# Output stage of a Fourier + SSD mixer: one y bank that also holds the sum of squares, three banks for decay exponents, Fourier rows first

## The chip, the core and the metric

The kernel runs on one core of one Trainium2 chip. The metric is device time in microseconds (us). A core has a matmul engine (TensorE, PE in the profile; its weight loads are PEld), three engines for everything else (VectorE is DVE, ScalarE is ACT, GpSimd is POOL) and a queue engine (SyncE, SP) that issues all DMAs of this kernel. Each engine works through its own list of instructions in a fixed order and waits on semaphores for the others. Matmul results go to PSUM, which has eight banks of 2 KB for each of the 128 partitions: a bank holds 512 float32 numbers per partition.

## The reference, cut to what matters

One layer works on 2048 latent tokens (and 256 context tokens ahead of them) of width 1024. One input projection feeds two groups: a Fourier group (512 channels, a two-dimensional DFT, a linear map, a SiLU gate) and an SSD group (1536 channels: 24 heads of 64 in four groups of six, a Mamba-2 scan in both directions, gated RMSNorm per group of 384 channels). Both are put side by side and multiplied by one output matrix. The change lies in the end of the SSD path and in the output product:

```python
lmat  = jnp.exp(segsum(a))                       # decay matrix of a chunk of 128 tokens, per head
y_diag = einsum(cb, lmat, xc)                    # inside the chunk
y_off  = einsum(cc, prev_states, exp(a_cum))     # from the state before the chunk
y = y_f + flip(y_b) + d_skip * xs
gated = y.reshape(b, l, g, r * p) * silu(zs)     # 4 groups of 384
gated = gated * rsqrt(mean(gated * gated, axis=-1, keepdims=True) + EPS)
ssd = gated.reshape(b, l, 1536) * norm_w
x = x + gate[:, None] * (concatenate([four, ssd], -1) @ w_out)
return rmsnorm(x, final_norm_w)
```

## The kernel before, in words

Earlier stages project the input, convolve, run the backward scan and the Fourier group, and leave their results in DRAM: the gated Fourier rows are in `fm_d`, the split output matrix in `wo_d`. The last stage, here called the output stage, takes the 16 chunks of 128 tokens in order, and in each chunk the four groups: 64 units, u = 4c + g. All matrix products of float32 data are made of three matmuls on a high and a low part (`split`: ScalarE copies the high part, another engine subtracts it for the low part, line 72).

A unit goes through six functions:

- `s1` loads the decay data and makes the decay exponents: in each of two halves of three heads two matmuls of 128x384, one for each direction, into two tiles `parg` (L1079); VectorE merges the second into the first under a mask (L1081), ScalarE takes the exponential (L1083), and after both halves VectorE multiplies by `cb` (L1084). The result is `w`.
- `s2` splits the running state `hf` and multiplies it with C: three matmuls into `pyo` (L1115 to L1117), scaled by VectorE into `ts` (L1119); GpSimd adds the stored backward part (L1120).
- `s3` makes the unit's contribution to the state, three matmuls into `pst4` (L1136 to L1138), and adds it to `hf` (L1141 on GpSimd, L1142 on VectorE). The last chunk has none.
- `s4` makes y, transposed, in the tile `py` of 128x384: six matmuls of x with `w` (L1151) and three transposes that add `ts` (L1154). VectorE gates it into `gt` (L1157), ScalarE squares (L1159), VectorE adds the three blocks into `s0` (L1161).
- `s5` makes the gated RMSNorm: a matmul of `s0` with a matrix of ones puts the sum of squares into `pn`, 128x128 (L1167, recorded as two passes); ScalarE takes logarithm, exponential and square (L1170, L1171, L1172), VectorE refines the reciprocal root in place in `pn` (L1173, L1174) and multiplies `gt` by it (L1176); `gt` is then split into `mh` and `ml` (L68 on ScalarE, L72 on GpSimd).
- `s6` makes the output product of the unit, 24 matmuls of 128x512 (L1210 to L1212): four blocks of rows (q) by two halves of the output (i) by three parts. Three blocks are the unit's SSD rows, the fourth its Fourier rows `fm`, which `fm_half` loads from `fm_d` for two units at a time into one buffer `fr` (L1186) and splits. `po0` and `po1` gather over the four units of a chunk. At g = 3 the gate (L1224), the residual (L1225, GpSimd), the sum of squares of the final norm (Square with an accumulator, L1227) and the store follow.

The program calls them for u = 0 ... 65 in this order: `s1(u+1)`, `s2(u+1)`, `s3(u)`, `s4(u)`, `s5(u-1)`, `s6(u-2)`. The units' order in the queues of the engines is not this one: a scheduler (`schedule_with_timeline_sim=True`, L1369) plays the program with its own durations and lists each engine's instructions as they come free. The lists are fixed before the run.

PSUM tiles come from the pool `ps2` by tag. A tile of a tag with one buffer can be written again when the last reader of the tile before it is done. Before the change the eight banks are: two for `parg`, two for `po0` and `po1`, two that `pyo` and `pst4` take in turn, one for `py`, one for `pn`.

Of the kernel before, what the change touches and what calls it, by code (L numbers as in the profile page):

```python
# [9 lines left out]
F32 = mybir.dt.float32  # L10
# [3 lines left out]
ALU = mybir.AluOpType  # L14
# [4 lines left out]
P = 128  # L19
# [30 lines left out]
def mixer_layer(ctx: ExitStack, tc: tile.TileContext, A: dict, out: bass.AP, taps=None):  # L50
    nc = tc.nc
    mm = nc.tensor.matmul

    def pool(name, bufs=1, space=None, stack=ctx, side=None):
        kw = {"space": space} if space is not None else {}
        if side is not None:
            kw["side"] = side
        if space != DRAM:
            kw["reuse_waits"] = "tile"
        return stack.enter_context(tc.tile_pool(name=name, bufs=bufs, **kw))  # L60

    def load(dst, src):
        return nc.sync.dma_start(out=dst, in_=src).ins
# [80 lines left out]
    ps = pool("ps01", stack=pps, space=PSUM)  # L144
# [7 lines left out]
    def main_psum():  # L152
        return ps.tile([P, 512], F32, name="pj", tag="mm", bufs=MAIN["bufs"])
# [202 lines left out]
    with ExitStack() as pu:  # L356
# [144 lines left out]
        for n2 in range(16):  # L501
            if n2 == 1:
                ctx_block()
            po = main_psum()
# [6 lines left out]
            with tc.issue_after(mu):  # L511
                if n2 in dt_work:
                    fn, i = dt_work[n2]
# [18 lines left out]
    with ExitStack() as pc_:  # L532
        ps = pool("psc", stack=pc_, space=PSUM)
# [164 lines left out]
    ps = pool("ps01b", stack=p1, space=PSUM)  # L698
# [72 lines left out]
    with ExitStack() as psc:  # L771
# [66 lines left out]
        for n, a in enumerate(seq):  # L838
            if n + AHEAD < len(seq):
                side.append((0.0, scan_prep(*seq[n + AHEAD])))  # L840
            dr, c, g = a
# [204 lines left out]
    ps = pool("ps2", space=PSUM)  # L1046
    fo["new"] = lambda: ps.tile([P, 512], F32, name="pft", tag="out", bufs=2)
    pre2 = preload(LNEXP)
    units = {}

    def s1(u):
        c, g = divmod(u, G)
        d = units[u] = {}
        if g == 0:
            sml = wa1.tile([P, 3, H], F32, name="sml4", tag="sml")
            load(sml, smf_d[:, c])
        else:
            sml = units[u - 1]["sml"]
        d["sml"] = sml
        r, l = rt[u % 2], lt[u % 2]  # L1060
        cs = slice(c * P, c * P + P)
        for dr in range(2):
            hsl = slice(dr * H + g * HG, dr * H + (g + 1) * HG)
            load(r[32 * dr + 12:32 * dr + 14, :].rearrange("o (h w) -> o h w", w=P).bitcast(F32),
                 cum_d[:, hsl, cs].bitcast(F32))
            for s in range(2):
                load(l[32 * dr + 6 * s:32 * dr + 6 * s + 6, dr].bitcast(F32), q_d[s, hsl, cs].bitcast(F32))
        cb = wa1.tile([P, P], F32, name="cb", tag="cb")
        load(cb, cb_d[c, :, g])
        chl = wa1.tile([P, 2, P], F32R, name="chl", tag="chl")  # L1070
        load(chl[:].bitcast(F32), chl_d[c, :, g].bitcast(F32))
        d["chl"] = chl
        w = wa1.tile([P, HG, P], F32, name="w", tag="w")
        for h2 in range(2):
            cols = slice(384 * h2, 384 * h2 + 384)
            pa = []
            for dr in range(2):
                po = ps.tile([P, 3, P], F32, name="parg", tag="arg", bufs=2)
                mm(po, l[:, dr], r[:, cols], start=True, stop=True)  # L1079
                pa.append(po)  # L1080
            nc.vector.copy_predicated(out=pa[0], mask=msk[:].unsqueeze(1).broadcast_to([P, 3, P]), data=pa[1])  # L1081
            with tc.issue_after(pre2):
                d["exp"] = nc.scalar.activation(w[:, 3 * h2:3 * h2 + 3], pa[0], AF.Exp).ins  # L1083
        nc.vector.tensor_tensor(out=w, in0=w, in1=cb[:].unsqueeze(1).broadcast_to([P, HG, P]), op=ALU.mult)  # L1084
        d["w"] = w

    for u in range(2):
        s1(u)
# [56 lines left out]
    def s4(u):  # L1145
        c, g = divmod(u, G)
        d = units[u]
        py = ps.tile([P, 3, P], F32, name="py", tag="yT", bufs=1)
        for h in range(HG):
            o = 64 * (h % 2)  # L1150
            mm(py[o:o + 64, h // 2, :], d["x"][:, h], d["w"][:, h], start=(h < 2), stop=False, skip_group_check=True)  # L1151
        tsf = d["ts"][:].rearrange("p h w -> p (h w)")
        for j in range(3):
            mm(py[:, j, :], tsf[:, j * P:(j + 1) * P], ident, is_transpose=True, start=False, stop=(j == 2),  # L1154
               skip_group_check=True)
        gt = wk.tile([P, 3, P], F32, name="gt", tag="gt")
        nc.vector.scalar_tensor_tensor(out=gt, in0=py, scalar=-1.0, in1=d["zs"], op0=ALU.mult, op1=ALU.mult)  # L1157
        sq = wk.tile([P, 3, P], F32, name="sq4", tag="sq", bufs=1)
        nc.scalar.activation(sq, gt, AF.Square)  # L1159
        s0 = wk.tile([P, P], F32, name="s0", tag="s0", bufs=1)  # L1160
        nc.vector.tensor_reduce(out=s0, in_=sq[:].rearrange("p j l -> p l j"), axis=AX.X, op=ALU.add)  # L1161
        d["gt"], d["sq"] = gt, s0

    def s5(u):
        d = units[u]
        pn = ps.tile([P, P], F32, name="pn", tag="misc", bufs=1)
        mm(pn, ones, d["sq"], start=True, stop=True)  # L1167
        rs = wk.tile([P, P], F32, name="rs4", tag="rs", bufs=1)
        tt = wk.tile([P, P], F32, name="tt", tag="tt", bufs=1)
        nc.scalar.activation(rs, pn, AF.Ln, bias=eps_t[:, 0:1], scale=1.0 / GW)  # L1170
        nc.scalar.activation(rs, rs, AF.Exp, scale=-0.5)  # L1171
        nc.scalar.activation(tt, rs, AF.Square, scale=math.sqrt(0.5 / GW))  # L1172
        nc.vector.scalar_tensor_tensor(out=pn, in0=pn, scalar=EPS * GW, in1=tt, op0=ALU.add, op1=ALU.mult)  # L1173
        nc.vector.scalar_tensor_tensor(out=pn, in0=pn, scalar=1.5, in1=rs, op0=ALU.subtract, op1=ALU.mult)  # L1174
        mx = d["gt"]
        nc.vector.tensor_tensor(out=mx, in0=mx, in1=pn[:].unsqueeze(1).broadcast_to([P, 3, P]), op=ALU.mult)  # L1176
        mh = wk.tile([P, 3, P], F32R, name="mh", tag="mh", bufs=2)
        ml = wk.tile([P, 3, P], F32R, name="ml", tag="ml", bufs=2)
        split(mh, ml, mx, nc.gpsimd)
        d["mh"], d["ml"] = mh, ml  # L1180
# [10 lines left out]
    def s6(u):  # L1191
        c, g = divmod(u, G)
        d = units.pop(u)
# [8 lines left out]
        fm = ost[c, g // 2]  # L1202
        if g % 2 == 1 and u + 1 < NU:
            fm_half(*divmod(u // 2 + 1, 2))
        ops = [(4 + 3 * g + j, d["mh"][:, j], d["ml"][:, j]) for j in range(3)] + [(g, fm[:, 0, g % 2], fm[:, 1, g % 2])]
        for i, q in [(i, q) for i in range(2) for q in range(4)] if (u > NU-2) else [(i, q) for q in range(4) for i in range(2)]:
                k, a, b = ops[q]
                wh, wl = wos[k]
                po = ost["po"][i]
                mm(po, a, wh[:, i], start=(g == 0 and q == 0), stop=False)  # L1210
                mm(po, a, wl[:, i], start=False, stop=False)  # L1211
                mm(po, b, wh[:, i], start=False, stop=(g == 3 and q == 3))  # L1212
# [27 lines left out]
        for i in range(2):  # L1240
            sl = slice(512 * i, 512 * i + 512)
            nc.vector.scalar_tensor_tensor(out=xr[i], in0=xr[i], scalar=rs[:, 0:1], in1=fnw[:, sl], op0=ALU.mult,
                                           op1=ALU.mult)
            store(out[c * P:(c + 1) * P, sl], xr[i])

    NU = NCH * G
# [126 lines left out]
```

## Time and profile before

| | |
|---|---|
| median of three runs | 1903.54 us (1899.87 to 1904.05) |
| the profiled execution | 1907.05 us, its span 1905.3 us |
| TensorE busy | 1810.8 us, 95% of the span |
| VectorE, GpSimd, ScalarE busy | 1259.1, 904.0, 874.9 us |
| granted TensorE clock, mean of the span | 0.978 |
| output stage: first `pn` to the end of the span | 1271.1 to 1905.3 us |
| first po with Fourier rows behind it to the last matmul | about 1306 to 1897 us |

A row of operations by line reads: line, engine, operation, output<-inputs, shape, count | busy time, mean ns of one | idle time of the engine just before them, and what ended most of it. A row of waits reads: who waited <- who released it: total us, times, longest. A row of windows reads: window, its length, busy time of TensorE with the number of instructions, the clock that it was granted, the share of the DMA engines, GB/s. A row of the timeline reads: start, duration, engine, line, operation, shape, and in brackets the idle time before it and what ended it. A row by one line of the program reads: shortest/median/longest ns, first start to last end. A span of 0.39 us for a matmul overlaps with its neighbours', since they are pipelined.

### The profile page before, as it was taken

How to read it: one execution, taken by the hardware profiler on the slowest of the kernel's cores; microseconds unless marked ns; L12 is line 12 of the kernel's file. 1: busy time of each engine (PE TensorE's matmuls, PEld its weight loads, DVE VectorE, ACT ScalarE, POOL GpSimd, SP SyncE). 2: the span in 40 equal slices, each digit the busy share in tenths (PEclk: the TensorE clock that was granted, in tenths of full speed). 3: DMA queues.
4: the chain of work that ended last, by engine and by line, in shares of the span. 5: the costliest groups of instructions: out<-in, count | busy, mean ns of one | idle time of the engine just before them, and what ended most of it. 6: DMA issues, size and time to landing. Idle time of an engine off the chain costs nothing.

```text
span 1905.3 us, 28132 instructions
## 1 busy us (share of the span) xinstructions
PE 1810.8 (95%) x9142; PEld 1495.8 (79%) x9142; DVE 1259.1 (66%) x1809; ACT 874.9 (46%) x1968; POOL 904.0 (47%) x791
## 2 busy tenths in 40 slices
PE   7989999999999999999999999957999999999997
PEld 3779988888888888788888877845778777777875
DVE  4744578888898887556666622334677777767865
ACT  4532244445445445347666643312444444434443
POOL 2320034223124133178788723235777777668742
PEclk9999999999999999999999999977999999999999
DMA  8332345445446245467777764786444444444441
GB/s 306 127 95 78 96 135 169 144 130 160 128 125 194 90 138 159 143 196 216 209 218 212 221 232 136 245 277 208 123 146 149 130 132 135 148 122 137 145 136 48
DMA packets 291332, 301.80 MB, mean 158 GB/s; under 512 B 34098, under 2 KB 242066, under 8 KB 290675
## 3 DMA queue, kind: packets, MB, share of 16 engines
q1 hardware_dynamic: 291186, 300.01, 50.6%
q8 instruction: 73, 1.20, 0.3%
q14 instruction: 73, 0.59, 0.1%
HBM read 196.82 MB, written 103.10 MB: 157 GB/s over the span
## 4 chain that ended last, share of the span: by engine, by line
PE 72%; DMA 9%; POOL 4%; DVE 3%; issue 2%; ACT 2%; SPq 1%; POOLq 0%; ACTq 0%; DVEq 0%
PE pj L178 11%; PE pj L177 11%; PE pj L176 11%; PE po L1212 6%; PE po L1210 6%; PE po L1211 6%; PE py L1151 2%; PE parg L1079 2%; POOL sl L72 2%; PE pj L508 1%; PE pj L509 1%; PE pj L510 1%; PE py L1154 1%; DMA ev<-in_wout 1%; PE ptr L569 1%
## 5 line engine op out<-in xcount | busy, mean ns | idle before, releaser
L178 PE MATMUL pj<-hh,wl 128*128 128x512 f32 x1152 | 453.9, 394 | 0.8 <-POOL wl L72 0.8
L176 PE MATMUL pj<-hh,wh 128*128 128x512 f32 x1152 | 450.7, 395 | 3.9 <-ACT img L68 2.1
L177 PE MATMUL pj<-hl,wh 128*128 128x512 f32 x1152 | 453.3, 393 | 0.0
L636 DVE SCALAR_TENSOR_TENSOR pacc<-img,c_convw,pacc 128x1024 f32<-128x1024 f32 x320 | 410.4, 1288 | 60.2 <-ACT pacc L633 50.7
L72 POOL TENSOR_TENSOR wl<-raw,wh 128x1024 fp32r<-128x1024 f32 x48 | 115.6, 2409 | 348.7 <-ACT wh L68 296.2
L178 PEld LDWEIGHTS pj<-hh,wl 128*128 128x128 f32 x1152 | 217.2, 189 | 48.3 <-issue 1.6
L176 PEld LDWEIGHTS pj<-hh,wh 128*128 128x128 f32 x1152 | 217.4, 189 | 46.7 <-ACT img L68 3.2
L177 PEld LDWEIGHTS pj<-hl,wh 128*128 128x128 f32 x1152 | 217.4, 189 | 40.3 <-issue 1.0
L807 ACT ACTIVATE xd<-xt,smb 128x64 f32<-128x64 f32 x384 | 100.9, 336 | 80.1 <-POOL yb L811 78.7
L1210 PE MATMUL po<-hl,mh 128*128 128x512 f32 x288 | 118.7, 412 | 1.0 <-DVE og L1224 0.6
L1211 PE MATMUL po<-hh,mh 128*128 128x512 f32 x288 | 115.0, 399 | 0.0
L1081 DVE COPY_PREDICATED parg<-msk,parg 128x384 f32<-128x384 uint8 x128 | 71.2, 556 | 65.9 <-PE parg L1079 65.4
L1212 PE MATMUL po<-hl,ml 128*128 128x512 f32 x288 | 110.6, 403 | 2.5 <-POOL ml L72 2.4
L1083 ACT ACTIVATE w<-parg 128x384 f32<-128x384 f32 x128 | 62.2, 486 | 108.3 <-DVE parg L1081 108.0
L72 DVE TENSOR_TENSOR xl<-xw,xh 128x384 fp32r<-128x384 f32 x76 | 63.7, 842 | 59.4 <-ACT xh L68 58.0
L1120 POOL TENSOR_TENSOR ts<-ts,yb 128x384 f32<-128x384 f32 x64 | 73.3, 1145 | 57.9 <-issue 30.4
L1079 PE MATMUL parg<-rt,lt 128*128 128x384 f32 x256 | 87.7, 371 | 11.8 <-DMA lt<-q_d 7.5
L72 POOL TENSOR_TENSOR ml<-gt,mh 128x384 fp32r<-128x384 f32 x64 | 68.2, 1065 | 58.9 <-ACT mh L68 55.5
L68 ACT ACTIVATE xh<-xw 128x384 fp32r<-128x384 f32 x136 | 70.0, 516 | 50.2 <-PE pst L1138 17.0
L1084 DVE TENSOR_TENSOR w<-w,cb 128x768 f32<-128x768 f32 x64 | 81.0, 1265 | 12.0 <-ACT w L1083 10.8
L72 POOL TENSOR_TENSOR sl<-ev,sh 128x512 fp32r<-128x512 f32 x32 | 42.4, 1324 | 89.6 <-DMA wo_d<-sl 36.0
L72 DVE TENSOR_TENSOR sl<-hbk,sh 128x384 fp32r<-128x384 f32 x64 | 60.0, 939 | 37.4 <-ACT sh L68 37.3
(388 smaller groups left out, 4131.9 us busy)
## 6 DMA issues: line engine op xcount, KB each, us to landing
raw<-in_win SPq DMA_DIRECT2D x48, 512.0 KB
xt<-xtok_d SPq DMA_DIRECT2D x80, 192.0 KB
xtok_d<-tk SPq DMA_DIRECT2D x48, 256.0 KB
zsT_d<-ev SPq DMA_DIRECT2D x48, 256.0 KB
yb_d<-yb SPq DMA_DIRECT2D x64, 192.0 KB
yb<-yb_d SPq DMA_DIRECT2D x64, 192.0 KB
zs<-zsT_d SPq DMA_DIRECT2D x64, 192.0 KB
xg<-xtok_d SPq DMA_DIRECT2D x64, 192.0 KB
```

The source lines that it names most:

```text
L72: (lo_engine or nc.vector).tensor_tensor(out=lo, in0=src, in1=hi.bitcast(F32), op=ALU.subtract)
L176: mm(po, wh[:, k], a, start=(k == 0), stop=False)
L177: mm(po, wh[:, k], b, start=False, stop=False)
L178: done["mm"] = mm(po, wl[:, k], a, start=False, stop=(k == KT - 1)).ins
L636: nc.vector.scalar_tensor_tensor(out=acc, in0=im[:, r0 + dy:r0 + dy + 16, dx:dx + GRID_W], scalar=tap(t), in1=acc, op0=ALU.mult, op1=ALU.add)
L807: nc.scalar.activation(xd[:, h], d["x"][:, h], AF.Copy, scale=smb[:, 3, c, g * HG + h:g * HG + h + 1])
L1079: mm(po, l[:, dr], r[:, cols], start=True, stop=True)
L1084: nc.vector.tensor_tensor(out=w, in0=w, in1=cb[:].unsqueeze(1).broadcast_to([P, HG, P]), op=ALU.mult)
L1120: nc.gpsimd.tensor_tensor(out=ts, in0=ts, in1=yb, op=ALU.add)
L1210: mm(po, a, wh[:, i], start=(g == 0 and q == 0), stop=False)
L1211: mm(po, a, wl[:, i], start=False, stop=False)
L1212: mm(po, b, wh[:, i], start=False, stop=(g == 3 and q == 3))
```

## The change

There are three edits in the output stage.

1. The two `parg` tiles of a half get tags of their own. The first direction's tile (`arg0`, which VectorE merges into and ScalarE reads) has two buffers, the second's (`arg1`, which only VectorE reads) has one: three banks in place of two.
2. The bank comes from `pn`. The `py` tile, so far 384 of the 512 columns of its bank, is made 512 wide, and `pn` of unit u becomes the fourth quarter of the `py` tile of unit u+1. The y tag still has one buffer. The last unit takes a fresh y tile for its `pn`.
3. In `s6` the Fourier rows are the first of the four blocks instead of the last; in the last unit both halves' Fourier rows come first, then the rest half by half.

```diff
@@ s1
-                po = ps.tile([P, 3, P], F32, name="parg", tag="arg", bufs=2)
+                po = ps.tile([P, 3, P], F32, name="parg", tag=f"arg{dr}", bufs=2 - dr)
                 mm(po, l[:, dr], r[:, cols], start=True, stop=True)
@@ s4
-        py = ps.tile([P, 3, P], F32, name="py", tag="yT", bufs=1)
+        py = d["py"] = ps.tile([P, 4, P], F32, name="py", tag="yT", bufs=1)
...
-        nc.vector.scalar_tensor_tensor(out=gt, in0=py, scalar=-1.0, in1=d["zs"], op0=ALU.mult, op1=ALU.mult)
+        nc.vector.scalar_tensor_tensor(out=gt, in0=py[:, :3], scalar=-1.0, in1=d["zs"], op0=ALU.mult, op1=ALU.mult)
@@ s5
-        pn = ps.tile([P, P], F32, name="pn", tag="misc", bufs=1)
+        pn = (units[u + 1]["py"] if u + 1 < NU else ps.tile([P, 4, P], F32, name="py", tag="yT", bufs=1))[:, 3]
         mm(pn, ones, d["sq"], start=True, stop=True)
...
-        nc.vector.tensor_tensor(out=mx, in0=mx, in1=pn[:].unsqueeze(1).broadcast_to([P, 3, P]), op=ALU.mult)
+        nc.vector.tensor_tensor(out=mx, in0=mx, in1=pn.unsqueeze(1).broadcast_to([P, 3, P]), op=ALU.mult)
@@ s6
-        ops = [(4 + 3 * g + j, d["mh"][:, j], d["ml"][:, j]) for j in range(3)] + [(g, fm[:, 0, g % 2], fm[:, 1, g % 2])]
-        for i, q in [(i, q) for i in range(2) for q in range(4)] if (u > NU-2) else [(i, q) for q in range(4) for i in range(2)]:
+        ops = [(g, fm[:, 0, g % 2], fm[:, 1, g % 2])] + [(4 + 3 * g + j, d["mh"][:, j], d["ml"][:, j]) for j in range(3)]
+        for i, q in ([(0, 0), (1, 0)] + [(i, q) for i in range(2) for q in range(1, 4)] if u > NU - 2
+                     else [(i, q) for q in range(4) for i in range(2)]):
```

Lines after 1202 stand one lower in the changed kernel. The scheduler makes new lists from this. Numbers behind a name in the following rows tell one tile of that name from another, so that a tile can be followed; `x6` is the count of equal rows.

TensorE in the middle of the stage, before: `pn` of unit 25 has its own tile, and `py_14639` of unit 26 follows further down.

```order
L1211 MATMUL po1_14670<-hh_85,mh_14527 128x512
L1167 MATMUL pn_14655<-s0_14515,c_ones_11274 128x128
L1079 MATMUL parg_14597<-rt1_11281,lt1_11283 128x384
L1115 MATMUL pyo_14848<-sh4_14849,chl_14823 128x384
L1116 MATMUL pyo_14848<-sl4_14850,chl_14823 128x384
L1117 MATMUL pyo_14848<-sh4_14849,chl_14823 128x384
L1151 MATMUL py_14639<-w_14456,xg_14474 64x128 x6
L1154 MATMUL py_14639<-c_ident_77,ts_14478 128x128 x3
```

The next `py` tile, unit 27's, is written some 30 rows further down. TensorE at the same place, changed: `pn` of unit 25 is written into `py_14614`, the tile of unit 26, and the next `py` tile in the same bank, `py_14726` of unit 27, is written five rows behind it.

```order
L1079 MATMUL parg_14807<-rt1_11281,lt1_11283 128x384
L1167 MATMUL py_14614<-s0_14491,c_ones_11274 128x128
L1115 MATMUL pyo_14929<-sh4_14930,chl_14904 128x384
L1116 MATMUL pyo_14929<-sl4_14931,chl_14904 128x384
L1117 MATMUL pyo_14929<-sh4_14930,chl_14904 128x384
L1079 MATMUL parg_14909<-rt0_11280,lt0_11282 128x384
L1151 MATMUL py_14726<-w_14569,xg_14587 64x128 x6
L1154 MATMUL py_14726<-c_ident_77,ts_14591 128x128 x3
```

So `pn` of a unit moved from ahead of the next unit's `py` to behind it, and the `py` of the unit after that follows after four to thirteen matmuls, depending on the unit.

ScalarE between the reading of the sum of squares and the high part of the normalised `gt`, changed, a unit with four matmuls in between (L68 is the copy of a high part, `sh4` of the state, `mh` of `gt`):

```order
L1170 ACTIVATE rs4_14157<-py_14140,eps_t_78 128x128
L1171 ACTIVATE rs4_14157<-rs4_14157 128x128
L68 ACTIVATE sh4_14705<-hf_6671 128x384
L1172 ACTIVATE tt_14158<-rs4_14157 128x128
L68 ACTIVATE mh_14165<-gt_14013 128x384
```

VectorE around the same steps, changed, for the `pn` of unit 26 (`py_14726` is its tile, `gt_14624` what it normalises):

```order
L1161 TENSOR_REDUCE s0_14740<-sq4_14738 128x128
L1142 TENSOR_TENSOR hf_6671<-hf_6671,pst4_14945 128x384
L1081 COPY_PREDICATED parg_14913<-msk8_11276,parg_14915 128x384
L1173 SCALAR_TENSOR_TENSOR py_14726<-py_14726,tt_14744 128x128
L1174 SCALAR_TENSOR_TENSOR py_14726<-py_14726,rs4_14743 128x128
L1176 TENSOR_TENSOR gt_14624<-gt_14624,py_14726 128x384
L1119 TENSOR_TENSOR ts_14928<-pyo_14929,sml4_14669 128x384
```

Other work of both engines stands between the steps on one sum of squares: a copy of the state's high part on ScalarE, the state's sum and a merge of exponents on VectorE.

TensorE where the stage begins, before: the sum of squares of unit 0 and the first output products stand around unit 1's `py`.

```order
L1151 MATMUL py<-w,xg 64x128 x6
L1154 MATMUL py<-c_ident,ts 128x128 x3
L1079 MATMUL parg<-rt_11281,lt_11283 128x384 x2
L1167 MATMUL pn<-s_11616,c_ones 128x128
L1151 MATMUL py<-w,xg 64x128 x6
L1154 MATMUL py<-c_ident,ts 128x128 x3
L1210 MATMUL po_11796<-hl,mh 128x512
L1211 MATMUL po_11796<-hh,mh 128x512
L1210 MATMUL po_11797<-hl,mh 128x512
```

The same place, changed:

```order
L1079 MATMUL parg<-rt_11281,lt_11283 128x384 x3
L1151 MATMUL py<-w,xg 64x128 x6
L1154 MATMUL py<-c_ident,ts 128x128 x3
L1151 MATMUL py<-w,xg 64x128 x6
L1154 MATMUL py<-c_ident,ts 128x128 x3
L1167 MATMUL py<-s_11616,c_ones 128x128
L1079 MATMUL parg<-rt_11280,lt_11282 128x384 x3
L1115 MATMUL pyo<-sh_11652,chl 128x384
L1116 MATMUL pyo<-sl_11653,chl 128x384
L1117 MATMUL pyo<-sh_11652,chl 128x384
```

The 18 output matmuls of unit 0's SSD rows no longer stand here: they come behind those of its Fourier rows.

## The prediction

> Times are microseconds of the profiled execution; u counts the 64 units of the output stage, four to a chunk.
>
> **What bounds the kernel now.** I read the page, then the output stage by windows, then what TensorE waited for there.
>
> ```profile
> span 1905.3 us, 28132 instructions
> PE 1810.8 (95%) x9142; PEld 1495.8 (79%) x9142; DVE 1259.1 (66%) x1809; ACT 874.9 (46%) x1968; POOL 904.0 (47%) x791
> ```
> ```profile
> 1306.00:1897.00 591.00, 573.62 (x3146) 0.99 0.44 131
> ```
> ```profile
> PE pst L1136 <- DVE ts L1119: 5.6, 9, 1.5
> PE po L1212 <- POOL ml L72: 2.4, 2, 1.7
> PE parg L1079 <- DVE parg L1081: 2.3, 2, 1.8
> PE py L1151 <- DVE w L1084: 1.8, 3, 0.8
> PE parg L1079 <- ACT w L1083: 0.4, 2, 0.3
> ```
>
> The windows row gives the stretch, its length, TensorE's busy time and its clock; the wait rows give total, times and longest of that stretch. From the first steady unit to the last matmul TensorE is busy 573.6 of 591.0: the stage is bound by its matmuls. Only 17.4 are idle, and the rows that the change could touch (parg on VectorE 2.3, on ScalarE 0.4, ml 2.4) make 5.1. With all waits gone the gain would end at 17. So the question is what new wait the shared bank brings.
>
> **The chain in the shared bank.** Last unit, nothing competing:
>
> ```profile
> 1885.15 0.38 PE L1167 MATMUL pn<-s,c_ones 128*128 128x128 f32 x2
> ```
> ```profile
> 1885.63 0.37 ACT L1170 ACTIVATE rs<-pn,eps_t 128x128 f32<-128x128 f32 x1 [2.08 <-PE pn L1167]
> 1886.03 0.31 ACT L1171 ACTIVATE rs<-rs 128x128 f32<-128x128 f32 x1
> 1886.37 0.31 ACT L1172 ACTIVATE tt<-rs 128x128 f32<-128x128 f32 x1
> ```
> ```profile
> 1886.72 0.30 DVE L1173 SCALAR_TENSOR_TENSOR pn<-pn,tt 128x128 f32<-128x128 f32 x1 [3.72 <-ACT tt L1172]
> 1887.05 0.30 DVE L1174 SCALAR_TENSOR_TENSOR pn<-pn,rs 128x128 f32<-128x128 f32 x1
> 1887.38 0.55 DVE L1176 TENSOR_TENSOR gt<-gt,pn 128x384 f32<-128x384 f32 x1
> ```
> ```profile
> L1167 PE MATMUL pn<-s,c_ones x128: 270/273/580, 1271.1 to 1885.3; 128*128 128x128 f32 x128
> L1176 DVE TENSOR_TENSOR gt<-gt,pn x64: 535/552/555, 1273.7 to 1887.4; 128x384 f32<-128x384 f32 x64
> ```
>
> From pn's start to the end of L1176, the last reader of pn, is 1887.93 - 1885.15 = 2.78: call it L. Pairing the 64 starts of L1167 with the 64 ends of L1176 (first and last in the two rows above), L is 2.73 at least, 4.24 in the median, 7.19 at most; the difference is queueing on ScalarE and VectorE. Now nothing waits for it: pn has its own bank, and the next use is a unit away.
>
> **The change, part by part.** With pn in the fourth quarter of a y tile and one y bank, the y tile of unit u+2 can't be written until L1176 of unit u has read the sum that lies in the tile of u+1. The first matmul of py(u+2) takes that wait, and with it everything behind it in TensorE's queue: the 24 po of a unit, parg, pst, pyo. In the changed order pn(u) stands behind py(u+1) and directly ahead of py(u+2). What lies between them is cover. Prices of it:
>
> ```profile
> 1361.85 0.39 PE L1211 MATMUL po<-hh,mh 128*128 128x512 f32 x1
> 1362.08 0.39 PE L1210 MATMUL po<-hl,mh 128*128 128x512 f32 x1
> 1370.11 0.33 PE L1116 MATMUL pyo<-sl,chl 128*128 128x384 f32 x1
> 1370.29 0.34 PE L1117 MATMUL pyo<-sh,chl 128*128 128x384 f32 x1
> ```
>
> Start to start, a 512-wide matmul costs 0.23 and a 384-wide one (pyo, pst, parg) 0.18. Counting the changed order, between pn(u) and py(u+2) stand 4 narrow ones (13 units: 0.70), 5 narrow (6: 0.88), 9 narrow (14: 1.58), 5 narrow and 6 wide (14: 2.28), 7 narrow and 6 wide (6: 2.69); the other nine are the entry and the end. Over the 59 units behind the entry the cover is 1.54 on average. A stall is L - 0.2 - cover (pn's own slot is 0.23, the handover about 0.04, as between tt's end and L1173's start above).
>
> How large L gets there I take from the changed orders of ScalarE and VectorE, with these means:
>
> ```profile
> L1081 DVE COPY_PREDICATED parg<-msk,parg 128x384 f32<-128x384 uint8 x121 | 67.3, 556 | 54.5 <-PE parg L1079 54.1
> L1142 DVE TENSOR_TENSOR hf<-hf,pst 128x384 f32<-128x384 f32 x57 | 31.2, 547 | 2.3 <-PE pst L1138 2.0
> L68 ACT ACTIVATE sh<-hf 128x384 fp32r<-128x384 f32 x58 | 30.1, 519 | 22.1 <-PE pyo L1117 18.0 <-DVE hf L1142 3.5
> L72 DVE TENSOR_TENSOR fm<-fr,fm 128x256 fp32r<-128x256 f32 x32 | 22.4, 701 | 17.7 <-ACT fm L68 17.1 <-DMA cb<-cb_d 0.5
> L1225 POOL TENSOR_TENSOR xr<-xr,og 128x512 f32<-128x512 f32 x30 | 41.5, 1382 | 13.1 <-DVE og L1224 13.1
> L1227 ACT ACTIVATE og<-xr 128x512 f32<-128x512 f32 x30 | 18.8, 628 | 11.7 <-POOL xr L1225 11.6
> ```
>
> With 4 narrow ones, a copy sh (0.52) stands between the chain's second and third activation: L = 2.78 + 0.55 = 3.3. With 9, the hf add and a parg copy stand ahead of L1173 and wait for pst and parg that follow pn (hf can start 1.15 after pn; 1.15 + 0.55 + 0.56 + 1.2 for the three VectorE steps = 3.5), and where the fm remainder (0.70) stands there too, 4.2. With 6 wide ones (a chunk's last unit) the Square L1227 (0.63 and its read of the sum) waits for GpSimd's xr (1.38) before the chain's second step: 4.25. Weighted: L = 3.8. Stall 3.8 - 0.2 - 1.54 = 2.06, times 59 = 122; the last two pn follow each other, 3 more: **+125**. Bounds: the quiet chain everywhere, by classes 13 x 1.89 + 6 x 1.71 + 14 x 1.01 + 14 x 0.31, some 10 for the end: +64; the median of before everywhere, 2.5 x 59: +150.
>
> TensorE also pays in clock:
>
> ```profile
> 1345.80:1349.21 3.41, 1.71 (x10) 1.00 0.41 139
> 1349.21:1352.62 3.41, 2.84 (x9) 0.50 0.85 272
> 1352.62:1356.04 3.42, 3.42 (x18) 0.50 0.57 171
> 1666.65:1670.06 3.41, 1.72 (x8) 1.00 0.24 70
> 1670.06:1673.48 3.42, 3.42 (x10) 0.50 0.48 131
> 1857.79:1861.20 3.41, 1.88 (x10) 1.00 0.41 119
> 1861.20:1864.61 3.41, 3.41 (x17) 1.00 0.07 19
> ```
> ```profile
> 1669.33 0.74 PE L1212 MATMUL po<-hl,ml 128*128 128x512 f32 x2 [1.67 <-POOL ml L72]
> ```
>
> The clock steps on a grid of 3.41. Twice a window only 1.7 busy was followed by a halved one; one 1.88 busy was not. One idle stretch of 1.67 was enough. A stall of 2.06 puts 1.65 or more into one window in (3.41 + 2.06 - 3.3)/3.41 = 0.64 of its positions, and a halved window costs half of 3.41: 0.64 x 1.7 x 59 = **+64**. Bounds: 0 (never) and, if every second window is halved too as at 1352.62, about +100. The Trainium skill ("TensorE: Matmul & The Clock Gate", section "HAM oscillation — how this bites in real kernels") gives the rule that idle gaps should stay under about 3.4 microseconds. By that rule alone these stalls would leave the clock alone; the trace disagrees with a halving after 1.67.
>
> The **third parg bank** and the **Fourier rows first** can remove at most the waits: all 16 of the stage vanish behind the longer ones (-16, with their halved windows (6.8 + 3.4)/2 = 5 more); neither end is below that. The instructions are the same in number and shape.
>
> At the **entry** before uses a hole:
>
> ```profile
> 1274.81 0.80 PE L1210 MATMUL po<-hl,mh 128*128 128x512 f32 x1 [0.39 <-ACT mh L68]
> 1280.10 0.39 PE L1212 MATMUL po<-hl,ml 128*128 128x512 f32 x1
> 1282.69 0.68 PE L1079 MATMUL parg<-rt,lt 128*128 128x384 f32 x2 [1.98 <-DMA lt<-q_d]
> ```
> ```profile
> 1301.57 0.42 SPq L63 DMA_DIRECT2D fr<-fm_d  x1
> ```
>
> Unit 0's 18 mh and ml matmuls run from 1274.81 to 1280.3, while SP's queue of loads holds the rest back. With the Fourier rows first they stand behind fr, issued at 1301.57 in the same place of SP's queue. They are paid later: 18 x 0.23 = **+4** (0 to 6).
>
> Sum: 1907.05 (the profiled run: 1905.3 and 1.75 around it) + 125 + 64 - 16 - 5 + 4 = 2079. The median of the runs shown is 3.5 lower: **2076**.
>
> **The rivals.** (B) *The chain stays quiet.* The stalls give the other engines slack, and the interposed copies are done early. For: last unit 2.78. Against: hf and copy wait for matmuls issued after pn. +64, clock only for the 19 units with 1.7 to 1.9 (0.56 x 1.7 x 19 = 18): 1907 + 64 + 18 - 17 = 1972, so 1968. (C) *The clock holds*, stalls falling across window borders as at 1857.79, with 1.75 idle in all. Against: 1666.65. 2079 - 64 = 2015, so 2012; that is the skill's rule. (D) *Not slower:* the wait is there but late work hides it, because parg and po flow better; it decides only if L - 0.2 falls under the cover in most units, and even 2.73 does so only for the 6 units with 2.69. Then 1907 - 16 - 5 + 4 = 1890, so 1886; or the change is a wash.
>
> **How the numbers follow.** Forecast 0.58, C 0.20, B 0.17, D 0.05. The forecast's own range is 2030 to 2150, its top from L = 4.24 (+26) and +36 on the clock. The range takes in C and nearly reaches B: 1975 to 2150. What a measurement can tell from no change is 0.2%, here 4. Slower 0.95, faster 0.04, same 0.01.
>
> **What would show it.** TensorE's waits in the output stage: py L1151 <- DVE gt L1176 at the top, some 60 times, 1 to 3 each, above 100 in sum. The time from pn to L1176's end: 3.8 if the queueing is right, under 3 for B. Windows of halved clock all over the stage, or none for C. First po behind 1301. Wrong altogether if py L1151 waits less than 30 in sum, or for something else.

## The result

The changed kernel takes 1991.27 us (median of 4 runs, 1988.66 to 1992.43) against 1901.88 for the kernel before in the same comparison: a ratio of 1.0461, interval 1.0446 to 1.0476. It is 4.6% slower. The forecast was 2076 with a range of 1975 to 2150; the time lies in the range and has the forecast sign, but only half of the forecast loss came.

The page of the changed kernel, span and busy time:

```profile
span 1990.4 us, 28131 instructions
PE 1828.7 (92%) x9142; PEld 1504.9 (76%) x9142; DVE 1240.3 (62%) x1809; ACT 873.3 (44%) x1968; POOL 894.8 (45%) x791
```

The span grew by 85.1 us, with the same 9142 matmuls. The output stage of the changed kernel by windows (the stretch that answers to 1306 to 1897 before; after the length stand the busy times of TensorE, its weight loads, VectorE, ScalarE and GpSimd with their numbers of instructions, then the clock, the share of the DMA engines and GB/s):

```profile
1312.00:1983.00 671.00, 589.20 (x3139) 465.95 (x3137) 400.69 (x773) 259.52 (x664) 384.62 (x373) 0.97 0.37 113
```

It is 80.0 longer than before (671.0 against 591.0). TensorE's idle time in it went from 17.4 to 81.8, +64.4; its busy time from 573.6 to 589.2, +15.6. The other 5.1 lie ahead of it and behind it. What TensorE waited for in that stretch (total, times, longest):

```profile
PE py L1151 <- DVE gt L1176: 50.5, 49, 1.9
PE pyo L1115 <- DVE hf L1142: 10.2, 20, 1.0
PE po L1211 <- DVE og L1225: 5.3, 15, 1.9
PE parg L1079 <- DVE parg L1081: 5.1, 9, 0.7
PE py L1151 <- issue: 4.6, 2, 2.4
PE py L1167 <- DVE gt L1176: 2.5, 1, 2.5
```

The first row did not exist before: the y of unit u+2 waits for the multiply of unit u, the last reader of the sum of squares in the shared bank. It holds 50.5 of the 64.4. The fifth row is the same wait at two places where the profile names no releaser (the y starts 0.1 after the end of L1176 there), and the sixth is the last unit's, together 7.1. The third row, one wait of 0.6 before, is the first output matmul of a chunk, which waits for the gate to read the chunk before out of its bank. Of the waits of the stage before, those of pst for ts, of po for ml and of y for w are gone; that of parg for the merge stayed and grew from 2.3 to 5.1, and that of pyo for hf from 0.8 to 10.2. One unit with four matmuls as cover, TensorE first, then ScalarE and VectorE (the timeline):

```profile
1656.13 0.39 PE L1167 MATMUL py<-s,c_ones 128*128 128x128 f32 x2
1656.27 0.42 PE L1115 MATMUL pyo<-sh,chl 128*128 128x384 f32 x1
...
1656.95 0.44 PE L1079 MATMUL parg<-rt,lt 128*128 128x384 f32 x1
1659.27 0.88 PE L1151 MATMUL py<-w,xg 128*64 128x128 f32 x12 [1.88 <-DVE gt L1176]
```
```profile
1656.15 0.42 ACT L68 ACTIVATE fm<-fr 128x256 fp32r<-128x256 f32 x1 [1.92 <-PE po L1213]
1656.55 0.37 ACT L1170 ACTIVATE rs<-py,eps_t 128x128 f32<-128x128 f32 x1
1656.95 0.31 ACT L1171 ACTIVATE rs<-rs 128x128 f32<-128x128 f32 x1
1657.17 0.51 ACT L68 ACTIVATE sh<-hf 128x384 fp32r<-128x384 f32 x1
1657.58 0.29 ACT L1172 ACTIVATE tt<-rs 128x128 f32<-128x128 f32 x1
```
```profile
1657.91 0.30 DVE L1173 SCALAR_TENSOR_TENSOR py<-py,tt 128x128 f32<-128x128 f32 x1 [0.18 <-ACT tt L1172]
1658.24 0.30 DVE L1174 SCALAR_TENSOR_TENSOR py<-py,rs 128x128 f32<-128x128 f32 x1
1658.57 0.55 DVE L1176 TENSOR_TENSOR gt<-gt,py 128x384 f32<-128x384 f32 x1
```

From pn's start (1656.13) the bank is held until L1176 ends (1659.12): 2.99. The copy `sh` stands between the second and the third activation, as the prediction said, but costs only 0.3 of its 0.51 there. TensorE's last matmul in between ends at 1657.39, and it stands still for 1.88.

The clock: two pairs of windows, on the grid on which the granted clock steps (last columns: clock, share of the DMA engines, GB/s):

```profile
1656.78:1660.20 3.42, 1.54 (x16) 0.97 (x15) 2.10 (x6) 1.60 (x6) 2.26 (x3) 1.00 0.67 223
1660.20:1663.61 3.41, 3.41 (x11) 2.84 (x12) 2.66 (x4) 1.38 (x3) 1.56 (x2) 0.50 0.79 229
1615.82:1619.23 3.41, 1.94 (x19) 1.67 (x20) 1.57 (x4) 1.47 (x4) 2.77 (x3) 1.00 0.59 193
1619.23:1622.64 3.41, 3.41 (x16) 2.78 (x15) 1.47 (x3) 0.53 (x1) 0.59 (x1) 1.00 0.71 205
```

Of these windows the one with 1.54 of busy time is followed by one at half clock, the one with 1.94 is not. In the records of the granted clock the stage spends 37.5 us at half clock, against 15.9 before (of which 5.7 are still the entry). With half of that time lost, it makes up 11 of the 15.6 more of busy time; this is an estimate from the two figures.

### The profile page after: what moved, and what is told of

It reads as the page before. It is cut to its first block, busy times and chain, and to the rows that moved or that the text cites. A ratio compares the mean times of both kernels' runs of the same rounds, so it can differ in the third digit from the quotient of the medians.

```text
span 1990.4 us, 28131 instructions
## 1 busy us (share of the span) xinstructions
PE 1828.7 (92%) x9142; PEld 1504.9 (76%) x9142; DVE 1240.3 (62%) x1809; ACT 873.3 (44%) x1968; POOL 894.8 (45%) x791
## 4 chain that ended last, share of the span: by engine, by line
PE 67%; DMA 9%; DVE 6%; issue 4%; ACT 4%; POOL 3%; SPq 1%; POOLq 0%; ACTq 0%; DVEq 0%
PE pj L178 10%; PE pj L177 10%; PE pj L176 10%; PE po L1211 6%; PE po L1212 6%; PE po L1213 6%; PE py L1151 3%; PE py L1154 2%; POOL sl L72 2%; DMA hl<-wo_d 1%; DVE gt L1176 1%; PE pj L508 1%; PE pj L509 1%; PE pj L510 1%; PE parg L1079 1%
## 5 line engine op out<-in xcount | busy, mean ns | idle before, releaser
L72 POOL TENSOR_TENSOR wl<-raw,wh 128x1024 fp32r<-128x1024 f32 x48 | 115.7, 2411 | 345.9 <-ACT wh L68 295.4
L1079 PE MATMUL parg<-rt,lt 128*128 128x384 f32 x256 | 94.0, 383 | 37.7 <-DVE yy L951 16.0
L1211 PE MATMUL po<-hl,mh 128*128 128x512 f32 x288 | 123.7, 429 | 0.0
L68 ACT ACTIVATE xh<-xw 128x384 fp32r<-128x384 f32 x136 | 70.3, 518 | 112.1 <-PE pst L1138 49.8
L1151 PE MATMUL py<-w,xg 128*64 128x128 f32 x768 | 59.5, 290 | 59.8 <-DVE gt L1176 50.5
L1161 DVE TENSOR_REDUCE s<-sq 128x128 f32<-128x384 f32 x64 | 38.0, 594 | 115.8 <-PE py L1167 111.1
L1151 PEld LDWEIGHTS py<-w,xg 128*64 128x64 f32 x768 | 44.8, 142 | 78.5 <-issue 61.2
L72 POOL TENSOR_TENSOR sl<-hf,sh 128x384 fp32r<-128x384 f32 x64 | 65.1, 1019 | 85.9 <-ACT sh L68 85.9
L72 DVE TENSOR_TENSOR xl<-xw,xh 128x384 fp32r<-128x384 f32 x76 | 64.1, 848 | 62.7 <-ACT xh L68 60.5
L72 POOL TENSOR_TENSOR xl<-xw,xh 128x384 fp32r<-128x384 f32 x60 | 62.3, 1038 | 87.6 <-ACT xh L68 87.4
L1079 PEld LDWEIGHTS parg<-rt,lt 128*128 128x128 f32 x256 | 49.7, 196 | 57.6 <-DVE parg L1081 19.2
L72 POOL TENSOR_TENSOR ml<-gt,mh 128x384 fp32r<-128x384 f32 x64 | 65.2, 1019 | 58.2 <-ACT mh L68 46.5
```

Source lines behind the costliest of these rows:

```text
L68: return nc.scalar.activation(dst, src, AF.Copy).ins
L72: (lo_engine or nc.vector).tensor_tensor(out=lo, in0=src, in1=hi.bitcast(F32), op=ALU.subtract)
```

## Experiments

Each run was compared with the kernel before on the same chip; its median was 1899.7 to 1901.9. Idle is TensorE's idle time from 1312 (1306 before, 1310 in chain_longer_early) to the last matmuls, from the windows; half clock is the time of it at the halved clock; cover is the mean of TensorE's matmuls between a sum of squares and the y that waits for it, counted in the list with 0.18 and 0.23 a matmul.

| kernel | median us | ratio to before, interval | cover | idle | half clock |
|---|---|---|---|---|---|
| before | 1901.9 | | 10.3, own bank | 17.4 | 15.9 |
| changed | 1991.3 | 1.0461, 1.0446 to 1.0476 | 1.59 | 81.8 | 37.5 |
| fourier_only | 1898.1 | 0.9984, 0.9972 to 0.9997 | 10.3, own bank | 14.8 | 13.7 |
| y_bank_only | 1985.6 | 1.0437, 1.0418 to 1.0456 | 1.81 | 75.7 | 37.5 |
| pn_early | 1889.6 | 0.9930, 0.9914 to 0.9945 | 6.30 | 8.5 | 0 |
| copy_out | 2247.0 | 1.1810, 1.1789 to 1.1831 | 0.26 | 192.6 | 286.7 |
| chain_longer | 2032.9 | 1.0700, 1.0667 to 1.0732 | 1.68 | 105.4 | 68.3 |
| chain_longer_early | 1907.0 | 1.0037, 1.0019 to 1.0056 | 6.41 | 24.7 | 6.8 |
| pn_middle | 1897.0 | 0.9975, 0.9964 to 0.9985 | 3.37 | 17.9 | 6.8 |
| early_two_banks | 1887.7 | 0.9924, 0.9911 to 0.9938 | 6.28 | 9.0 | 0 |
| own_bank_early | 1908.6 | 1.0043, 1.0030 to 1.0055 | 14.1, own bank | 14.1 | 0 |
| edge_only | 1892.1 | 0.9956, 0.9944 to 0.9968 | 13.7, own bank | 9.6 | 3.4 |
| early_two_y | 1888.8 | 0.9938, 0.9925 to 0.9951 | 6.22, two y banks | 7.9 | 0 |
| two_s0 | 1986.9 | 1.0453, 1.0440 to 1.0467 | 1.61 | 79.4 | 37.5 |

### Which of the three edits

Theory: the shared y bank makes the whole loss. Rivals: the new order of the output product, or the single bank of the second direction's exponents. Two kernels take the edits apart.

**fourier_only** is the kernel before with the third edit:

```diff
-        ops = [(4 + 3 * g + j, ...) for j in range(3)] + [(g, fm[:, 0, g % 2], fm[:, 1, g % 2])]
+        ops = [(g, fm[:, 0, g % 2], fm[:, 1, g % 2])] + [(4 + 3 * g + j, ...) for j in range(3)]
```

> The kernel before with the third edit alone (Fourier rows first); the banks stay as before. Theory (the shared y bank is the whole loss: the y of unit u+2 waits for the multiply L1176 of unit u): the sum of squares keeps its own bank, so the loss is gone; what is left is the entry (about +5: the first output matmul waits for the Fourier load near 1303) against the short waits for ml (2.4 in before). 1898 to 1912, likeliest 1905, no wait of y for L1176. Rival 1 (the order of the output product makes the loss: the first output matmul of a chunk now waits 5.3 for the gate reads): 1940 or more. Rival 2 (the single second-direction parg bank makes the loss): also near 1905 here.

Measured 1898.1, at the lower end of what was expected, and just faster than before. The third edit makes no loss.

**y_bank_only** is the changed kernel with the two old `parg` banks:

```diff
-                po = ps.tile([P, 3, P], F32, name="parg", tag=f"arg{dr}", bufs=2 - dr)
+                po = ps.tile([P, 3, P], F32, name="parg", tag="arg", bufs=2)
```

> The changed kernel with parg back at one tag with two banks, so that one bank lies empty: the sum of squares in the y bank, the Fourier rows first. Theory: the wait is the same, the list of TensorE gives it a little more cover (1.81 instead of 1.59 us of matmuls between pn and the y after next, on average), so 1975 to 1995, with 35 to 55 of waits of y for L1176. Rival 1 (product order): about 1991 as well. Rival 2 (the parg banks make the loss): back to 1900 to 1910.

Measured 1985.6: nearly the whole loss with the second edit and the third. So the loss needs the shared y bank. The second edit without the third was not run, so whether it also needs the Fourier rows first is not shown. The waits of the stage:

```profile
PE py L1151 <- DVE gt L1176: 27.1, 43, 1.1
PE parg L1079 <- DVE parg L1081: 19.5, 30, 1.9
PE po L1211 <- DVE og L1225: 11.6, 14, 1.9
PE py L1151 <- issue: 5.8, 5, 1.5
```

The wait of y for L1176 was expected at 35 to 55 and is 27.1 in its row; with the rows in which the y starts within 0.2 of the end of L1176, though the profile names another releaser or none, it is 33.9, and the last unit's wait adds 2.5. Against the changed kernel 14.4 more stand on the merge of exponents and 6.3 more on the gate. With TensorE's list stopped once a unit, what it waits for next only moves between rows: all of the stage's idle time is 75.7 here and 81.8 in the changed kernel.

### Hold against cover

Theory: the bank is held for some 3.4 from pn on, and what TensorE has to do until the y that needs the bank is only 1.6, because pn stands late in its list. If so, the same banks with pn early must lose nothing.

**pn_early** adds an order edge; `issue_after` puts the instructions in its block behind the named one in their engine's list:

```diff
-        mm(pn, ones, d["sq"], start=True, stop=True)
+        pns[u] = mm(pn, ones, d["sq"], start=True, stop=True).ins
...
+                with ExitStack() as st:
+                    if u + 1 < NU and q >= 1:
+                        st.enter_context(tc.issue_after(pns[u + 1]))
                     mm(po, a, wh[:, i], start=(g == 0 and q == 0), stop=False)
```

> The changed kernel with all three edits, and an order edge for TensorE: of a unit's output matmuls all but the first six stand behind the sum of squares of the unit after it. Now pn stands about 2 us of matmuls behind the y in whose tile it lies, and 6.3 us (5.0 to 7.0) ahead of the y that waits for it; in the changed kernel these were 7.1 and 1.6. Theory (hold of 3.4 against cover): 6.3 is above every hold but a few, so the wait of y for L1176 falls from 50 to under 5, the idle time of the stage to 10 to 25, and the time to 1892 to 1908, likeliest 1900. If the bank is lost whatever the order (the hold grows with the cover, because the chain then runs against more work on ScalarE and VectorE): 1940 to 1990. Rivals 1 and 2: no change, 1980 to 2000.

Measured 1889.6, 102 us faster than the changed kernel and 0.7% faster than before; that is 2 below the range that was expected, and the idle time of 8.5 is below its range too. The stage and all its waits (from L1079 on the lines stand one higher here, so that L1176 is L1177):

```profile
1312.00:1880.00 568.00, 559.51 (x3136) 450.23 (x3134) 415.34 (x772) 255.65 (x664) 394.16 (x374) 1.00 0.44 134
```
```profile
PE parg L1080 <- DVE parg L1082: 4.4, 12, 1.0
PE py L1168 <- DVE gt L1158: 2.9, 6, 0.7
PE pst L1138 <- POOL xl L72: 0.2, 1, 0.2
```

No y waits for the multiply, and the clock is never halved in the stage. Yet the hold, the time from pn's start to the multiply's end, is longer here, 4.1 to 4.4 in the three largest groups of units instead of 3.0 to 3.9; that the chain now meets more work on ScalarE and VectorE is the likely reason, and not shown. The hold was never the trouble by itself; its place was.

**pn_middle** is pn_early with the edge put later (`q >= 3` in place of `q >= 1`):

> pn_early with the edge put later: of a unit's output matmuls eighteen, not six, may stand ahead of the next sum of squares. Only the place of pn in TensorE's list differs: cover 3.37 on average (3.0 to 3.5) between pn and the y that waits. Theory (stall = hold + 0.14 - 0.24 - cover): with the hold of 3.4 that the changed kernel shows, nothing; with the 4.2 that pn_early shows, 0.7 x 59 = 43. So 1889 to 1932, likeliest 1905, with 5 to 30 of waits of y for L1176: between the two, as the cover is. If early or late is all that counts (a scheduler's side effect elsewhere): near 1890 or near 1990.

Measured 1897.0, in the range and 8 below the likeliest value. With 3.37 of cover y waits for the multiply 6.9 us in sum:

```profile
PE parg L1080 <- DVE parg L1082: 7.5, 14, 2.0
PE py L1152 <- DVE gt L1177: 6.9, 8, 2.0
```

From 1.59 over 3.37 to 6.30 of cover the time goes 1991, 1897, 1890: the loss ends where the cover comes near the hold, which is 3.5 in the mean in pn_middle.

### The length of the chain

**chain_longer** does the third activation three times, with the same result:

```diff
         nc.scalar.activation(tt, rs, AF.Square, scale=math.sqrt(0.5 / GW))
+        nc.scalar.activation(tt, rs, AF.Square, scale=math.sqrt(0.5 / GW))
+        nc.scalar.activation(tt, rs, AF.Square, scale=math.sqrt(0.5 / GW))
```

> The changed kernel with the third activation of the chain (L1172, 0.31 us, 0.33 with the handover) done three times over with the same result: the chain in the shared bank is 0.66 longer, ScalarE has 42 us more work in 64 units, of 1117 idle. Cover in the new list 1.68 on average (1.59 in the changed kernel). Theory (the chain is on the path, because the y of unit u+2 waits for its end): 59 x (0.66 - 0.09) = +34, and 0 to 15 for more halved clock windows: 2018 to 2045. If the time of the changed kernel came from something else than the chain's length: 1985 to 2000.

Measured 2032.9, 41.6 above the changed kernel and in the range, though not in the parts that were expected: its stage has 24 us more idle time, where 34 were put, and 16 more busy time. The first waits of its stage (L1178 is the multiply here):

```profile
PE py L1151 <- DVE gt L1178: 52.1, 46, 1.9
PE py L1151 <- issue: 21.8, 12, 2.9
```

The two rows together went from 55.1 to 73.9; all idle time from 81.8 to 105.4, and the time at half clock from 37.5 to 68.3.

**chain_longer_early** does the same in pn_early:

> The same three-fold activation in the kernel with the early sum of squares (pn_early). Hold there 4.2, now 4.9; cover 5.0 to 7.5, 6.4 on average. Theory: the chain is not on the path, so the same 0.66 costs nothing or a few us where the cover is 5.0: 1888 to 1900. If ScalarE's work or the chain's length cost as such: 1920 or more.

Measured 1907.0, 17.4 above pn_early and a miss: 1888 to 1900 were expected, and 1920 or more for the other cause. The y's wait for the multiply did not come back, but another grew, from 2.9 in pn_early:

```profile
PE py L1168 <- DVE gt L1158: 20.4, 16, 2.5
```

This is pn itself (L1168 here) waiting until VectorE has gated the y in whose tile it is written. The shared bank has a wait at both ends of pn: the next y behind it, and the gating ahead of it. Of the 20.4, 18.5 stand in eleven units, one in a chunk, in which VectorE works through the final norm (L1249) and the low part of the Fourier rows (L72) ahead of the gating (L1158), as here:

```profile
1464.89 2.25 DVE L1249 SCALAR_TENSOR_TENSOR xr<-xr,ry,c_fnw 128x512 f32<-128x512 f32 x2
1467.06 1.04 DVE L72 TENSOR_TENSOR fm<-fr,fm 128x256 fp32r<-128x256 f32 x1
1468.03 0.54 DVE L1158 SCALAR_TENSOR_TENSOR gt<-py,zs 128x384 f32<-128x384 f32 x1
1468.63 0.49 PE L1168 MATMUL py<-s,c_ones 128*128 128x128 f32 x2 [1.86 <-DVE gt L1158]
```

The lists of this kernel and of pn_early differ at this place (there a merge of exponents stands between the final norm and L72), so it is not shown that the longer chain as such makes VectorE late. What the run shows is that the early pn has little room at its other end, and that the longer chain does not bring back the wait of y.

### Letting the bank go earlier

**copy_out** copies the sum of squares out of the bank first, and the chain works on the copy:

```diff
         mm(pn, ones, d["sq"], start=True, stop=True)
+        pc = wk.tile([P, P], F32, name="pc4", tag="pc4", bufs=1)
+        nc.vector.tensor_copy(out=pc, in_=pn)
+        pn = pc
...
```

> The changed kernel with one operation more in each unit: VectorE copies the sum of squares out of the shared bank (128x128), and the rest of the chain works on the copy. The bank is then held only from pn to the end of the copy: quiet some 0.42 + 0.33 = 0.75 us, more where the copy queues on VectorE. The list answers with less cover, 0.26 us on average instead of 1.59. Theory (stall = hold - 0.2 - cover): with holds of 0.9 to 1.4 stalls of 0.45 to 0.95, 27 to 55 in sum, and few halved clock windows, since single waits stay under 1: 1930 to 1965, and y waits for the copy, not for L1176. If what costs is the handover from VectorE to TensorE as such and not the length of the hold: 1985 to 2000.

Measured 2247.0: a miss by 282 from the top of the range. The waits on TensorE, and one on VectorE:

```profile
PE parg L1079 <- DVE parg L1081: 78.3, 59, 1.6
PE py L1151 <- DVE pc L1169: 46.6, 56, 1.0
PE pyo L1115 <- DVE hf L1142: 30.4, 52, 0.8
PE po L1214 <- ACT mh L68: 20.3, 22, 3.6
```
```profile
DVE s L1161 <- PE py L1167: 254.4, 60, 7.4
```

The wait of y is what the formula gave, 46.6 where 27 to 55 were expected. But the scheduler put pn straight ahead of the y that waits for it, and three more waits came that the formula doesn't hold: VectorE stands 254 us at the reduction of the next unit, because s0 has one buffer and a late pn has not read it yet, and the merge and the state's sum stand behind the reduction in VectorE's list, as does the chain's first step on VectorE, which waits for the third activation 44.5 us more. TensorE stops three times a unit instead of once, and the clock is halved for 286.7 us. Releasing a bank earlier is worth nothing if the list then puts its user right behind the release.

In the changed kernel the same wait stands on VectorE, at less than half:

```profile
DVE s L1161 <- PE py L1167: 109.2, 32, 5.1
```

**two_s0** gives s0 two buffers there (`bufs=2` in place of `bufs=1`):

> The changed kernel with two buffers for s0, the tile that the sum of squares reads (one buffer so far). In the changed kernel VectorE's reduction of the next unit waits 109 us in sum for pn, since s0 can't be written before pn has read it, and hf, the merges and the gating queue behind it on VectorE. Cover in the list as before, 1.61. Theory: that queue is where the waits of pyo for hf (10.2) and of parg for the merge (5.1) come from; they go, the wait of y for L1176 stays at 45 or more: 1970 to 1985. If they have another cause: 1985 to 1998.

Measured 1986.9, 4 faster than the changed kernel, in the range of the other cause. The reduction no longer waits for pn, but TensorE's waits stay:

```profile
PE py L1151 <- DVE gt L1176: 46.8, 49, 1.6
PE pyo L1115 <- DVE hf L1142: 9.0, 21, 0.9
```

So VectorE's stand at the reduction is not needed for the changed kernel's other waits. It was not tried whether two buffers would mend copy_out; that its other waits come from the reduction's stand is argued from the order of VectorE's list, and not shown.

### What the banks and the edge are worth by themselves

**early_two_banks** is pn_early with `parg` back at two banks and one bank empty:

> pn_early without the third parg bank: parg again one tag with two banks, one bank of the eight empty. It prices the bank that the change is named for, with the loss out of the way. Theory (TensorE bound by its matmuls, waits for the merges of the exponents 2.7 in before): 1889 to 1896, the third bank is worth 0 to 6. If the third bank is what makes pn_early 12 us faster than before: 1898 to 1905.

Measured 1887.7, 1 below the range that was expected, against 1889.6 with three banks. With the loss out of the way the third bank for the exponents, after which the change is named, is worth nothing that can be measured.

**early_two_y** gives the empty bank to y (`tag="yT", bufs=2`):

> early_two_banks with the empty bank given to y (two y banks; the sum of squares still in the fourth quarter). Theory: no y waits any more in early_two_banks, so a second bank is worth nothing: 1884 to 1892. If waits that the idle column does not show come from the single y bank: 1875 to 1883.

Measured 1888.8: as expected, nothing either.

**edge_only** is the kernel before with the order edge, its own banks and its own product order (the y tile is 512 wide, its fourth quarter unused):

> The kernel before with the order edge alone: its banks, its product order (Fourier rows last). It prices the edge without all three edits. Theory: the edge spreads the output matmuls behind the sums of squares and takes the short waits (pst for ts 5.6, ml 2.4, merges 2.7) and their halved windows; Fourier rows first made -3 alone. 1888 to 1900, likeliest 1893. If the edge works only with the Fourier rows ahead of it, as the six matmuls that may go first: 1898 to 1905.

Measured 1892.1, faster than before by 0.44% (0.32 to 0.56): most of the gain of pn_early comes without any of the three edits.

**own_bank_early** is early_two_banks with pn in a bank of its own, which adds the Fourier order to edge_only:

> early_two_banks with the sum of squares back in a bank of its own: the banks are those of the kernel before, Fourier rows first, and the order edge for TensorE. Between pn and the y two units on stand 14.1 us of matmuls. Theory (the shared bank costs nothing when its hold is covered, and gains nothing either; the order edge makes the gain): 1884 to 1893, the same as early_two_banks within 4. If sharing the bank helps in some way of its own: 1896 or more.

Measured 1908.6, a miss: slower than before, and 21 slower than the kernel with the shared bank. That is the range in which sharing the bank would help by itself; but edge_only, with the same banks, takes 1892.1, so the bank of its own is not enough to explain it. The clock is not halved, and the stage's idle time of 14.1 is only 5 more than in early_two_banks. The rest hides in the busy column:

```profile
1312.00:1899.00 587.00, 572.89 (x3134) 445.14 (x3133) 391.34 (x769) 266.39 (x660) 394.25 (x372) 1.00 0.43 130
1312.00:1878.00 566.00, 557.05 (x3118) 448.80 (x3116) 404.00 (x769) 250.45 (x661) 393.53 (x372) 1.00 0.44 134
```

The first row is own_bank_early, the second early_two_banks: 16 us more busy for nearly the same matmuls at full clock. Adding up TensorE's time from each matmul's start to the next one's, from the first output matmul of unit 3 to the end, gives 20 us more, of which 5 are idle time. It lies behind the `parg` (63.3 against 52.6, but 8.5 of the difference is idle time), the `pst` (37.3 against 30.9) and the output matmuls (355.7 against 348.7), while `pyo` takes 5 less. One place of many: a `pst` stands right behind a `parg` 48 times here and 14 times in early_two_banks. In 24 of the 48 it starts late, 0.55 after the `parg` in the median of these, where its slot is 0.18; in the other kernel it never does. Of such a delay only what outlasts the matmul's own run of 0.33 shows as idle time. Why this list costs more than that of edge_only, which has the same banks, was not settled and stays open.

## Why the prediction was right, and where its sizes were off

**Bound by matmuls; all of the old waits worth at most 17.** Right. pn_early takes the idle time down to 8.5 and gains 12 (0.7%); the third bank gives none of it.

**The wait of y for L1176 as the new bound.** Right, in mechanism, place and name; y_bank_only, pn_middle, pn_early and chain_longer show it from four sides. It tops the list with 49 waits of 0.3 to 1.9, 29 of them under 1, where "some 60 times, 1 to 3 each, above 100 in sum" stood. With the two rows of the same kind it is 57.6 in sum.

**The stall of 2.06 per unit, +125: the step that was mis-sized.** What came is 64.4 of idle time net of the 17.4 before, where 125 - 16 = 109 was put. One part is the hold. Taking L from the orders of ScalarE and VectorE with whole durations gave 3.8; over the units from the third on it is 3.42. That is 22 of the 45 that are missing. Class by class (predicted, measured): four narrow ones 3.3 and 3.00, nine narrow ones 3.5 or 4.2 and 3.40, five narrow and six wide ones 4.25 and 3.80. An operation that stands in the list between two steps costs only what of it isn't done while the step ahead is under way: `sh` took 0.3 there instead of 0.55.

For the rest, take the 57 units from the fourth to the 60th. From pn's start to the start of the y that waits, TensorE takes 204.2 in sum. The slots of the list are 104.1 of it, the wait for L1176 53.6, other waits in between 19.8; the last matmul runs 12.0 past its slots before its wait begins, and the others stand 14.7 further apart than their slots. The prediction's formula calls all of this stall but the first; the last two count as busy time, and the other waits stand in rows of their own. So the time that TensorE lost at these places, 100 in 57 units or 1.76 a unit, is near the 2.06, and the wait for L1176 is only half of it.

Rival B, the quiet chain, priced the stalls at +64 and the whole at 1968; the truth lies between it and the forecast, and outside the forecast's own range of 2030 to 2150. The stated range holds the time only because it was drawn wide enough for the rivals. The chain is neither quiet (2.78) nor as slow as the sum of the lists. One class is misnamed, without effect on the sum: what is called 7 narrow and 6 wide are 10 narrow and 4 wide matmuls in the trace, which gives the 2.69, so the cover goes up to fourteen matmuls and not thirteen.

**The clock, +64 (or +59 net): mechanism right, size wrong.** The stage has 37.5 at half clock against 15.9, which costs 11 more. The prediction let every stall of 2.06 push a window under 1.8 busy in 0.64 of its positions, some 38 windows; 10 were halved. Seven of them come from the 13 units with four narrow matmuls, where the wait is 1.88 and falls into one window. The other three are one unit with two waits in its window (0.53 and 1.19), a wait of 1.88 for the gate, and the last unit's 2.5. In size, 11 is nearer to rival C, where the clock holds, than to 64; as a rule C fails, since single waits of 1.88 were followed by a halved window. The Trainium skill ("TensorE: Matmul & The Clock Gate", section "HAM oscillation — how this bites in real kernels") asks only for idle gaps under about 3.4. The trace disagrees with that rule here too.

**The third parg bank: -16 at most with all old waits.** Most of them are gone from the stage, as put, but the wait for the merge, which the bank was to shorten, rose from 2.3 to 5.1. In pn_early, where a gain could have shown, the bank gives nothing.

**The entry: +4.** Right, as far as one place can tell: the 24th output matmul is followed by the 25th at 1314.0 instead of 1309.8, with the first one at 1304.0, behind the load of the Fourier rows.

**Rival D, that other work hides the wait,** is what pn_early makes true by moving one instruction. The prediction had it decide once hold - 0.2 falls under the cover; pn_middle, with a cover near the hold, is where it does.

## What to carry to other kernels

When two tiles share a bank, look in the engines' lists for how much work stands between the first write of the held part and the next use of the bank, and compare it with the time until the last reader is done: here 1.6 against 3.4 cost 4.6%, and 6.3 against 4.2 cost nothing, with the same code but for one order edge. A scheduler that lists instructions as they come free can put a short but urgent matmul behind long work that is merely ready; naming that order takes no bank. And a change of buffers changes every list, so price it with the list held as still as possible, or the list is what gets measured (copy_out, own_bank_early).

## What the runs showed of the hardware

In the records of the granted clock it steps on a grid of 3.41 us. With the windows laid on that grid, a full-clock window with little busy time is mostly followed by a halved one, and the border lies near half a window. In the changed kernel ten of the stage's full-clock windows were followed by a halved one, with 1.48 to 1.70 busy; of the thirteen with less than 2.3 busy that were not, eleven had 1.94 or more, and the two others 1.58 and 1.72. In two_s0 the eleven halved ones had 1.81 at most and the others 1.82 at least, but for one with 1.61 at the stage's end. The border is not sharp: in chain_longer_early windows with 1.58 and 1.64 were followed by full clock, and in y_bank_only one with 1.95, in fourier_only one with 2.61 by half clock. So busy time by itself does not decide.

In copy_out, whose idle time comes in three short waits a unit, the border lay at 2.07. That the profile's busy time counts the run-out of each matmul ahead of a wait would fit this, and is not shown. Several short waits halve the clock as one long one does: in 57 of the 58 windows there that were followed by a halved one no single wait took more than 1.6 of the window, and in seventeen none took more than 1. That kernel spent 286.7 of its 926 us there at half clock.
